# A hybrid decoder layer on one core: the last four gates as block pairs, and joined edits at the seams, in attention, at the feed-forward opening and at the last tokens

## The chip, the core and the metric

The kernel runs on one core of a Trainium2 chip. The metric is the device time of one execution in microseconds (us): the span from the first to the last instruction and the little that lies around it. The engines are named as the profile names them: PE is the matrix engine (TensorE) and PEld its weight loads, DVE the vector engine, ACT the scalar engine, POOL GpSimd, and SP the engine whose queue issues most DMA transfers; some are issued from ACT's queue.

## The reference, cut to what matters

The layer takes a prompt of 1024 tokens and eight single sample tokens; the kernel puts them side by side as 1032 columns (`TT`) of 1024 features. Everything is float32.

```python
def mixer_block(xn, mem_k, mem_v, ...):
    sc_b, sc_c, sc_x, z, xbc, dt_raw, q, gates = split(xn @ w_in)
    y_a = (sc_b * causal_conv(sc_c * sc_x)) @ w_sc_out                 # 1024 -> 1024
    xs, bm, cm = split(silu(causal_conv(xbc) + ssm_conv_b))            # 2048, 4x128, 4x128
    y_ssd, ssm_new = ssd_fn(xs, softplus(dt_raw + bias), a, bm, cm, s0)
    y_b = group_rmsnorm((y_ssd + ssm_d * xs) * silu(z)) @ w_ssm_out    # 2048 -> 1024
    y_c = softmax(q @ mem_k / 16) @ mem_v @ w_attn_o                   # 4 heads of 256, 256 memory tokens
    g_a, g_b, g_c = split(sigmoid(gates))                              # 3 x 1024
    return (g_a * y_a + g_b * y_b + g_c * y_c) @ w_merge_o, states

x = x + mixer_block(rmsnorm(x), ...)
x = x + (silu(h @ w_gate) * (h @ w_up)) @ w_down                       # h = rmsnorm(x), hidden size 2816
y = rmsnorm(x)
```

For the prompt `ssd_fn` is a scan over eight chunks of 128 tokens for each of four groups of eight heads; for each sample token it is one step of the recurrence from a given state, and its attention reads keys and values from a cache of its own. Outputs are `y`, the memory's keys and values, and the convolution and scan states.

## The kernel before, in words

**Layout and products.** Activations lie with 128 features on the partitions and the 1032 columns along the free dimension. A projection is computed in blocks of 128 output features. Each float32 operand is split into a rounded high part (an ACT copy) and a remainder (a DVE subtraction, `split_act` for activations, `weights` for weights), and each product of two operands is three products of TensorE: high by high, high by low, low by high.

**A plain block** (`gemm`, product at L195) covers the columns in three strips of 344. With 1024 input features (eight steps of `k`) that is 8 x 3 x 3 = 72 products. Between steps of `k` it calls `tick()`, which runs the next entry of the queue `pend`; `pace[0]` says how many entries a block takes. So other work (the scan, the attention) is emitted piece by piece between the products of plain blocks. `run_next` takes the next entry of its queues and, before it runs that one, issues the weight load of the one behind it if that is a `Step`.

**A pair of blocks** (`strassen`, products in `st_prod` at L240, two strips of 258 columns) computes two blocks of 128 features together with seven half-size products in place of eight: 168 products. Its inputs are sums and differences of quarter blocks of the activations (the forms B11, T1, nT2, B21, T3, B22, T4) and of the weights; the sums of the weights are made on DVE (`sa`, `sb`) and split (`st_split`) inside the pair. `st_early` computes the part with B11 and B21 of several blocks ahead of the other forms; their pairs then only need the rest.

**Stages in time.** The opening normalizes the input (to about 62 us). Three plain blocks follow (`xbc_tile(16)`, `xbc_tile(20)`, `z_step`), then the `z` pairs; beside these `pend` holds the memory's norm (`mem_rms`), its transposes (`mem_t`, half by half) and its keys and values (`kv_block`), 110 to 280 us. Until 971 us come the pairs of `xbc`, of the gates 0 to 19 (`gate_pair`) and of the short convolution, with steps of the sample recurrence beside them. `again` recomputes some activation forms from the stored input; the last pair, gates 18 and 19, has `plain` as its hook, which loads the first scan group and turns the forms back into plain activations.

Then the scan (971 to 1312 us). Its pieces fill `pend`, and the plain blocks that run beside it are twelve `fillers`, eight of `q` (`q_step`) and four of the gates 20 to 23 (`gate_step`, a plain block, a sigmoid on ACT, a store to `gt_d`), followed by the first eight output blocks (`outs`: `w_sc_out`, names `wo00` to `wo07`). `pace[0]` is the number of pieces divided by these twenty blocks; a chunk is `first` (transposes and masks), `second` (products `po`, L923, and `py`, L931, with the DVE steps at L927, L936 and L940) and `third` (state product `pss`, L949). After the last chunk of a group come its gating by `zs` (`z_pieces`, L1029), the sums for its norm (L1037) and the norm itself.

Beside attention (1370 to 1608 us) run the other sixteen output blocks: `wo10` to `wo17` and `wo20` to `wo27`, the two halves of `w_ssm_out`. Ahead of each run of eight, `out_in` loads the eight input blocks and splits them. An output block (`out_part`) loads its gate, multiplies the product by it (L1304), loads the sum so far (`mg_d`), adds and stores it. The attention's pieces, five for each block, are scores (`psa`, L1494) and softmax (L1415) for the prompt, probabilities transposed (`psp`, L1508), output (`a_out`), and the same for each sample (`s_query`, `s_keys`, `s_scores`: DVE products with sums, L1403, and so on). Then `w_attn_o` (`wo30` to `wo37`, to 1699 us) with the last gating and adding, `w_merge_o` (L1653, to 1795 us), the norm, five early blocks of the feed-forward part (`st_early`: gate 0, up 0, gate 2, up 2, gate 4; all but the first are stored in `e_d`), the pairs of its hidden features (to 2247 us), and the down projection. Its last part is done by columns: strips of 384, 384 and 264 columns (products at L1854 to L1856), each followed by `finish` for its three tiles of tokens: transposes (`psy`, L1830), squares on ACT, the scaling (L1839) and the store (L1840). The last tile holds the eight samples alone.

**What sets the order.** The text of the kernel is emitted once, and a list scheduler decides each engine's order from the dependences, under the marks that the text sets: `in_turn` keeps the load and split of weights in turn, and `tc.issue_after` puts an instruction behind a named one. Tiles come from pools with a fixed number of buffers, so a tile's load waits until an earlier holder is read. Loads by SP are issued in their order: a load that waits for its buffer holds those behind it.

## Time and profile before

| | us |
|---|---|
| runs of before | 2517.67, 2515.51, 2518.59 |
| their median | 2517.67 |
| the profiled execution, its own time | 2517.93 |
| its span, first to last instruction | 2516.0 |
| mean granted TensorE clock | 0.995 of full speed |

Busy time by stage of the profiled execution, for the stages that the prediction does not show:

| stretch, us | what | length | PE | DVE | ACT |
|---|---|---|---|---|---|
| 0 to 62 | opening | 62 | 44.81 | 37.90 | 40.01 |
| 280 to 971 | pairs ahead of the scan | 691 | 689.49 | 497.31 | 330.09 |
| 1608 to 1699 | `w_attn_o` | 91 | 90.48 | 44.96 | 22.06 |
| 1699 to 1795 | `w_merge_o` | 96 | 95.41 | 52.66 | 33.68 |
| 1842 to 2247 | hidden pairs | 405 | 404.28 | 217.74 | 138.59 |
| 2247 to 2463 | down projection | 216 | 215.84 | 70.25 | 36.55 |

How to read the rows: the lines of stretches in the prediction give start and end, length, then busy time and number of records for PE, PEld, DVE, ACT and POOL, the granted clock (1.00 is full speed), the busy share of the DMA engines and GB/s. A row of the chain of waits gives where a run of equal work starts, how long it holds the chain, its engine, and what it is. A wait row names who waits, for whom, then the time lost in us, how often, and the longest. A group's row gives line, engine, operation and tile, out<-in, then busy time and mean ns of one. A PE record is one pass of one product; a full float32 product leaves two records. "PE busy" is time in which a product is under way, and the waits of an engine that is not the bottleneck cost nothing.

### The profile page before, as it was taken

The numbers are of one execution on the slowest core, as the hardware profiler recorded it, in microseconds if no ns is written. First come the engines' busy times: TensorE is split into PE (matmuls) and PEld (weight loads), VectorE is DVE, ScalarE is ACT, GpSimd is POOL, SyncE is SP. The second block draws the span as 40 slices with busy tenths as digits, with TensorE's granted clock in tenths as the row PEclk, the third lists the DMA queues.
The fourth block names the chain that finished last, engine by engine and source line by source line (L and its number), as shares of the span: only waits on it lengthen the run. The fifth ranks groups of instructions, "written<-read, shape, count | busy, mean of one in ns | idle before, by whom it ended". The sixth has DMA issues, their size and how long they took to land.

```text
span 2516.0 us, 44833 instructions
## 1 busy us (share of the span) xinstructions
PE 2457.5 (98%) x18642; PEld 2391.0 (95%) x18642; DVE 1521.8 (60%) x2588; ACT 1040.5 (41%) x1679; POOL 139.1 (6%) x163
## 2 busy tenths in 40 slices
PE   7999999999999999999999999999999999999998
PEld 5999999999999998999989888999999999999998
DVE  6754586777677774776877762545775445463326
ACT  6553455353544535556544341213443333341102
POOL 0300000000000000321220000000000000000000
PEclk9999999999999999999999999999999999999999
DMA  6344434344344456666868987935442222273211
GB/s 201 101 147 156 126 102 152 110 128 125 110 135 135 127 157 195 193 209 226 299 214 281 319 262 231 316 120 160 139 143 85 85 69 93 71 248 128 76 34 68
DMA packets 348154, 394.71 MB, mean 157 GB/s; under 512 B 15414, under 2 KB 284838, under 8 KB 347943
## 3 DMA queue, kind: packets, MB, share of 16 engines
q1 hardware_dynamic: 328798, 338.90, 42.9%
q10 hardware_dynamic: 19153, 52.96, 5.6%
q8 instruction: 146, 2.39, 0.4%
q14 instruction: 57, 0.47, 0.1%
HBM read 283.57 MB, written 108.45 MB: 156 GB/s over the span
## 4 chain that ended last, share of the span: by engine, by line
PE 86%; DVE 6%; DMA 5%; ACT 2%; issue 1%; SPq 0%; DVEq 0%; ACTq 0%; POOL 0%
PE po L195 11%; PE pd L195 9%; PE ps_q L195 4%; PE pm L1653 4%; DMA kc<-in_cache_mem_k_dram 1%; PE py L931 1%; PE ps_g L195 1%; PE pss L949 1%; PE po L923 1%; PE ps_z L195 1%; PE X17m L240 1%; PE C3m L240 1%; PE G18m L240 1%; PE Z14m L240 1%; PE C6m L240 1%
## 5 line engine op out<-in xcount | busy, mean ns | idle before, releaser
L1795 DVE TENSOR_TENSOR x<-pd,x 128x1032 f32<-128x1032 f32 x24 | 29.6, 1232 | 130.7 <-PE pd L195 130.7
L878 ACT ACTIVATE r<-r,acum 128x128 f32<-128x128 f32 x256 | 78.8, 393 | 4.9 <-DMA r<-ac_d 4.5
L1304 DVE TENSOR_TENSOR gt<-po,gt 128x1032 f32<-128x1032 f32 x24 | 29.5, 1229 | 52.9 <-PE po L195 52.8
L910 POOL TENSOR_TENSOR xdd<-xdt,decst 128x512 f32<-128x512 f32 x32 | 44.7, 1397 | 295.1 <-DVE xdt L906 295.1
L649 DVE SCALAR_TENSOR_TENSOR ax<-u,prm,ax 128x1024 f32<-128x1024 f32 x44 | 56.3, 1280 | 0.1
L819 ACT ACTIVATE st<-st,es 128x128 f32<-128x128 f32 x128 | 41.7, 400 | 24.7 <-DMA st<-in_state_ssm_dram 19.9
L904 DVE TENSOR_TENSOR r<-r,cbm 128x1024 f32<-128x1024 f32 x32 | 39.0, 1218 | 8.8 <-ACT r L879 8.5
L821 DVE SCALAR_TENSOR_TENSOR st<-sr,dts,st 128x128 f32<-128x128 f32 x128 | 40.1, 345 | 0.4
L903 ACT COPY bT<-bp 128x128 f32<-128x128 f32 x32 | 8.5, 266 | 76.9 <-DVE cbm L901 76.9
L931 PE MATMUL py<-r,xdt 128*64 128x128 f32 x512 | 35.9, 283 | 4.2 <-issue 4.2
L927 DVE TENSOR_TENSOR yt<-po,ea 128x512 f32<-128x512 f32 x28 | 19.3, 691 | 34.0 <-PE po L923 34.0
L940 DVE SCALAR_TENSOR_TENSOR x<-x,dpar,yt 128x128 f32<-128x128 f32 x128 | 36.2, 345 | 0.2
L931 PEld LDWEIGHTS py<-r,xdt 128*64 128x64 f32 x512 | 28.0, 139 | 8.5 <-issue 5.1
L825 DVE SCALAR_TENSOR_TENSOR sr<-st,sr 128x128 f32<-128x128 f32 x128 | 35.3, 286 | 1.1
L879 ACT ACTIVATE r<-r 128x1024 f32<-128x1024 f32 x32 | 33.9, 1060 | 0.7
L949 PE MATMUL pss<-xdd,bT 128*128 128x512 f32 x64 | 33.7, 608 | 0.0
L1582 DVE TENSOR_TENSOR gt<-po,gt 128x1032 f32<-128x1032 f32 x8 | 9.9, 1233 | 38.4 <-PE po L195 38.4
L1660 DVE TENSOR_TENSOR x<-pm,xT 128x516 f32<-128x516 f32 x16 | 11.1, 695 | 35.8 <-PE pm L1653 35.8
L962 POOL TENSOR_TENSOR s<-s,cdec 128x512 f32<-128x512 f32 x28 | 32.2, 1149 | 0.5 <-DVE s L955 0.4
L1403 DVE SCALAR_TENSOR_TENSOR kc<-kc,qb 128x256 f32<-128x256 f32 x64 | 23.9, 419 | 13.7 <-DMA qb<-qs_d 7.9
L923 PE MATMUL po<-bc,s 128*128 128x128 f32 x224 | 29.5, 275 | 0.0
L923 PEld LDWEIGHTS po<-bc,s 128*128 128x128 f32 x224 | 28.4, 191 | 0.0
(9099 smaller groups left out, 8891.8 us busy)
## 6 DMA issues: line engine op xcount, KB each, us to landing
gt<-gt_d SPq DMA_DIRECT2D x32, 516.0 KB
r<-ac_d SPq DMA_DIRECT2D x32, 512.0 KB
mg_d<-gt SPq DMA_DIRECT2D x24, 516.0 KB
mg<-mg_d SPq DMA_DIRECT2D x24, 516.0 KB
xs_d<-ax ACTq DMA_DIRECT2D x22, 516.0 KB
hr<-h_d SPq DMA_DIRECT2D x22, 516.0 KB
gt_d<-G ACTq DMA_DIRECT2D x20, 516.0 KB
x<-xs_d SPq DMA_DIRECT2D x16, 516.0 KB
```

The lines of the kernel that those rows point to most:

```text
L195: PE.matmul(ps[:, n, :CW], wt[:, ks], x[:, n * CW : (n + 1) * CW], start=(k == 0 and i == 0), stop=(k == nk - 1 and i == 2),)
L240: PE.matmul(ps[:, n, :HC], wt[:, ks], x[:, n * HC : (n + 1) * HC], start=(start and kt == 0 and i == 0), stop=(kt == 3 and i == 2), skip_g ...
L649: V.scalar_tensor_tensor(acc[:, :T], u[:, j : j + T], w[j], acc[:, :T], op0=ALU.mult, op1=ALU.add)
L819: S.activation(st[:, i], st[:, i], AF.Copy, scale=es[:, g * 4 + i, b : b + 1])
L821: V.scalar_tensor_tensor(st[:, i], rb, dts[:, g * 4 + i, b : b + 1], st[:, i], op0=ALU.mult, op1=ALU.add)
L878: S.activation(r[:, j, :], r[:, j, :], AF.Relu, scale=-1.0, bias=acum[:, c, h : h + 1])
L904: V.tensor_tensor(r, r, bc(cbm.unsqueeze(1), [P, HPG, P]), op=ALU.mult)
L910: G.tensor_tensor(b3(xdd, HPG), b3(xdt, HPG), bc(decst[:, c, hs].unsqueeze(2), [P, HPG, 64]), op=ALU.mult)
L923: PE.matmul(po[:, t * P : (t + 1) * P], state["s"][:, t * P : (t + 1) * P], bcg[1][:, cs], start=True, stop=True,)
L931: PE.matmul(py[hp : hp + 64, (h // 2) * P : (h // 2 + 1) * P], xdt[:, h * 64 : (h + 1) * 64], r[:, (h % 2) * 4 + h // 2, :], start=True, s ...
L949: PE.matmul(pss, bT, xdd, start=True, stop=True)
L1653: PE.matmul(ps[:, n, :HC], wt[:, ks], x[:, half * HT + n * HC : half * HT + (n + 1) * HC], start=(k == 0 and i == 0), stop=(k == KD - 1 an ...
```

## The change

- **Gates 20 to 23** are no longer plain blocks beside the scan. `gate_pair(20)` and `gate_pair(22, plain)` follow `gate_pair(18)` ahead of the scan (18 and 20 now run before `again`); `gate_step` is gone. The scan has sixteen blocks beside it, so its pace is higher, and `marks` in `gemm` becomes a list, so that two pieces can fall on one step of `k`.
- **Seams between runs of blocks.** The inputs of the next run of output blocks are loaded and split inside the last block of the run before it (`out_ahead` puts a function into `seam`, which `gemm` calls at each `k`). Stores of an output block's result are put off to the second step of the next block (`owed`). The scan's pool moves to the right side of the memory.
- **Attention.** For the first half of `w_ssm_out` an output block now only copies the raw product (ACT) and stores it in `yr_d` from ACT's queue; for the second half it adds the raw product, multiplies the sum by the gate once and stores it in `yg_d`; it is added to the merged sum in the `w_attn_o` blocks. The sample's score steps (L1403) are ordered behind the scaled maximum of the softmax last emitted, and the sample's pieces start one place earlier, with an empty place in the middle. `q_rows` is called at once in place of through `pend`. The weights of `w_attn_o` are loaded one block ahead.
- **Seams in front.** In `strassen` the copy of the first quarter (`o11`) stands behind the split of the weights' sum; the memory's pieces get one more empty place behind `mem_rms`, and the two halves of `mem_t` become one piece; the weights of `xbc_tile(20)` are issued ahead of `xbc_tile(16)`.
- **Feed-forward opening.** A sixth early block, up 4, joins `st_early`.
- **Last tokens.** The strip of 264 columns becomes two: columns 896 to 1031 (token tile 7 and the samples), then columns 768 to 895 (tile 6), each followed by its own `finish`.

The diff, cut:

```diff
@@ -178,6 +178,9 @@
+    seam, owed = [], []
     def gemm(w, acts, name, width=P, off=0):
@@ -185,9 +188,14 @@
         pace[1] += pace[0] - n
-        marks = {nk * i // n for i in range(n)}
+        marks = [nk * i // n for i in range(n)]
+        between = seam.pop() if seam else None
         for k, (ah, al) in enumerate(acts):
-            if k in marks:
+            if between is not None:
+                between(k)
+            if k == 1 and owed:
+                owed.pop()()
+            for _ in range(marks.count(k)):
                 tick()
@@ -296,8 +304,7 @@
             prod(pa, wA, 0, "B11", True)
-            S.copy(h3(o11), hv(pa))
-        if early is not None:
+        else:
             tick()
@@ -308,6 +315,7 @@
             wS = st_split(sa, f"{nm}S")
+            S.copy(h3(o11), hv(pa))
         if ready is None:
@@ -353,12 +361,14 @@
     mg_d = dram("mg_d", [KD, P, TT])
+    yr_d = dram("yr_d", [KD, P, TT])
+    yg_d = dram("yg_d", [KD, P, TT])
     xs_d = dram("xs_d", [24, P, TT])
...
     h_d = dram("h_d", [NF, P, TT])
-    e_d = dram("e_d", [4, P, TT])
+    e_d = dram("e_d", [5, P, TT])
     q_d = dram("q_d", [8, P, TT])
@@ -701,15 +711,6 @@
-    def gate_step(i):
-        def s():
-            ps = proj(C_G + i * P, f"g{i}")
-            t = ev_tile(f"g{i}")
-            S.activation(t3(t), flat(ps), AF.Sigmoid)
-            S.dma_start(gt_d[i], t[:, :TT])
-        return [Step(wblock(w_in, C_G + i * P), f"wg{i}", s)]
     def xbc_conv(ct, u, name):
@@ -722,9 +723,9 @@
-    def xbc_tile(ct, name, ps=None):
+    def xbc_tile(ct, name, ps=None, w=None):
         if ps is None:
-            ps = proj(C_XBC + ct * P, name)
+            ps = gemm(w, xn, "ps_" + name)
         u = ev_tile("u" + name)
@@ -1138,9 +1139,10 @@
+    w_c0 = weights(wblock(w_in, C_XBC + 20 * P), "wC0")
     xbc_tile(16, "B0", ps_b0)
     make_forms(0)
-    xbc_tile(20, "C0")
+    xbc_tile(20, "C0", w=w_c0)
     make_forms(2)
@@ -1212,8 +1214,8 @@
     mem_load()
-    pend.extend([None, mem_rms])
-    pend.extend(lambda m=m, half=half: mem_t(m, half) for m in range(2) for half in range(2))
+    pend.extend([None, mem_rms, None])
+    pend.extend(lambda m=m: [mem_t(m, half) for half in range(2)] for m in range(2))
     pend.extend(lambda j=j, q=q: kv_block(j, q) for j in range(8) for q in range(2))
@@ -1245,6 +1247,8 @@
     assert not steps
+    gate_pair(18)
+    gate_pair(20)
     rb = ev_tile("rb")
@@ -1268,18 +1272,16 @@
-    gate_pair(18, plain)
+    gate_pair(22, plain)
     st_stack.close()
...
-    pool["ssd"] = ssd.enter_context(tc.tile_pool(name="ssd", bufs=2))
+    pool["ssd"] = ssd.enter_context(tc.tile_pool(name="ssd", bufs=2, side="right"))
     fillers = deque()
...
         fillers.extend(q_step(i))
-    for i in range(20, 24):
-        fillers.extend(gate_step(i))
@@ -1291,32 +1293,61 @@
     def out_in(src):
-        acts.clear()
-        for k in range(KD):
+        acts[:] = split
+        split.clear()
+        for k in range(len(acts), KD):
             if not ahead:
...
-    def out_part(w, m, gate, more, nm):
-        gt = ev_tile(f"gt{nm}")
-        SY.dma_start(gt[:, :TT], gt_d[gate])
+    def out_ahead(src):
+        for k in range(2):
+            out_load(src, k)
+        def between(k):
+            if k > 1:
+                split.append(split_act(ahead.popleft()[:, :TT], f"b0{k - 2}"))
+                out_load(src, k)
+        seam.append(between)
+    def out_part(i, m, w, src, nxt):
+        nm = f"{i}{m}"
+        if m == 0:
+            out_in(src)
+        if i != 1:
+            gt = ev_tile(f"gt{nm}")
+            SY.dma_start(gt[:, :TT], gt_d[(0, 8, 8)[i] + m])
+        if i == 2:
+            t = ev_tile(f"yr{nm}")
+            SY.dma_start(t[:, :TT], yr_d[m])
+        if m == KD - 1:
+            out_ahead(nxt)
         ps = gemm(weights(wblock(w, m * P), f"wo{nm}"), acts, f"po{nm}")
-        V.tensor_mul(t3(gt), flat(ps), t3(gt))
-        if more:
-            t = ev_tile(f"mg{nm}")
-            SY.dma_start(t[:, :TT], mg_d[m])
-            V.tensor_add(gt[:, :TT], gt[:, :TT], t[:, :TT])
-        SY.dma_start(mg_d[m], gt[:, :TT])
+        if i == 0:
+            V.tensor_mul(t3(gt), flat(ps), t3(gt))
+            owed.append(lambda: SY.dma_start(mg_d[m], gt[:, :TT]))
+        elif i == 1:
+            t = ev_tile(f"yr{nm}")
+            S.copy(t3(t), flat(ps))
+            S.dma_start(yr_d[m], t[:, :TT])
+        else:
+            V.tensor_tensor(t3(t), flat(ps), t3(t), op=ALU.add)
+            V.tensor_mul(t[:, :TT], t[:, :TT], gt[:, :TT])
+            owed.append(lambda: SY.dma_start(yg_d[m], t[:, :TT]))
+    split = []
     outs = deque()
-    for i, (src, w) in enumerate(
-        ((sc_d, a["w_sc_out"][0]), (yb_d, a["w_ssm_out"][0, 0:D]), (yb_d[8:16], a["w_ssm_out"][0, D : 2 * D]))
-    ):
-        outs.append(lambda src=src: out_in(src))
+    ins = ((sc_d, a["w_sc_out"][0]), (yb_d, a["w_ssm_out"][0, 0:D]), (yb_d[8:16], a["w_ssm_out"][0, D : 2 * D]), (at_d, None))
+    for i, (src, w) in enumerate(ins[:3]):
         outs.extend(
...
                 wblock(w, m * P), f"wo{i}{m}",
-                lambda w=w, m=m, i=i: out_part(w, m, (0, 8, 8)[i] + m, i > 0, f"{i}{m}"),
+                lambda i=i, m=m, w=w, src=src, nxt=ins[i + 1][0]: out_part(i, m, w, src, nxt),
             )
@@ -1331,15 +1362,13 @@
     while fillers or pend:
-        if len(fillers) == 2 and not ahead:
-            for k in range(2):
-                out_load(sc_d, k)
+        if len(fillers) == 1:
+            out_ahead(sc_d)
         run_next(fillers, outs)
     assert not fillers
-    pend.append(q_rows)
-    run_next(outs)
+    q_rows()
     flush()
@@ -1400,17 +1429,18 @@
                 c = slice(h * 256, (h + 1) * 256)
-                V.scalar_tensor_tensor(
-                    kc[:, c], kc[:, c], 1.0, qbs[b][:, c], op0=ALU.mult, op1=ALU.mult,
-                    accum_out=sc_s[:, m, b, h : h + 1],
-                )
+                with tc.issue_after(slot[0]):
+                    V.scalar_tensor_tensor(
+                        kc[:, c], kc[:, c], 1.0, qbs[b][:, c], op0=ALU.mult, op1=ALU.mult,
+                        accum_out=sc_s[:, m, b, h : h + 1],
+                    )
...
             V.tensor_reduce(mx[:npart, :n], sv, axis=AX.X, op=ALU.max)
-            V.tensor_scalar(mx[:npart, :n], mx[:npart, :n], -1.0 / 16.0, None, op0=ALU.mult)
+            ins = V.tensor_scalar(mx[:npart, :n], mx[:npart, :n], -1.0 / 16.0, None, op0=ALU.mult)
             for i in range(n):
@@ -1418,8 +1448,8 @@
             for i in range(n):
-                ins = V.tensor_scalar(pr[:, i, :], pr[:, i, :], sm[:npart, i : i + 1], None, op0=ALU.mult)
-            return ins
+                V.tensor_scalar(pr[:, i, :], pr[:, i, :], sm[:npart, i : i + 1], None, op0=ALU.mult)
+            return ins.ins
@@ -1496,7 +1527,7 @@
             heads[h][2][l2] = pr
-            return softmax(pr, ps, 2, P, nm)
+            slot[0] = softmax(pr, ps, 2, P, nm)
@@ -1539,9 +1570,9 @@
         for b in range(NS):
-            at_ = 4 + 5 * b
+            at_ = 3 + 5 * b
             for i, fs in enumerate(
-                ([(s_query, b), (s_keys, b, 0)], [(s_keys, b, 1)], [(s_scores, b, 0)], [(s_scores, b, 1)])
+                ([(s_query, b), (s_keys, b, 0)], [(s_keys, b, 1)], [], [(s_scores, b, 0)], [(s_scores, b, 1)])
             ):
@@ -1562,7 +1593,9 @@
         ph2 = ctx.enter_context(tc.tile_pool(name="ph2", bufs=1))
-        while outs:
+        assert not pend
+        outs.append(Step(wblock(a["w_attn_o"][0], 0), "wo30", None))
+        while len(outs) > 1:
             run_next(outs)
@@ -1574,11 +1607,17 @@
     for m in range(KD):
+        w = weights(wblock(a["w_attn_o"][0], m * P), f"wo3{m}")
+        if m + 1 < KD:
+            loaded[f"wo3{m + 1}"] = load_raw(wblock(a["w_attn_o"][0], (m + 1) * P), f"wo3{m + 1}")
         merged.append(big(f"mg{m}"))
         SY.dma_start(merged[m], mg_d[m])
+        yg = ev_tile(f"yg{m}")
+        SY.dma_start(yg[:, :TT], yg_d[m])
         gt = ev_tile(f"gt3{m}")
         SY.dma_start(gt[:, :TT], gt_d[16 + m])
-        ps = gemm(weights(wblock(a["w_attn_o"][0], m * P), f"wo3{m}"), acts, f"po3{m}")
+        ps = gemm(w, acts, f"po3{m}")
+        V.tensor_add(merged[m], merged[m], yg[:, :TT])
         V.tensor_mul(t3(gt), flat(ps), t3(gt))
@@ -1686,7 +1725,7 @@
     blocks = []
-    for i, (nm, j) in enumerate((("g", 0), ("u", 0), ("g", 2), ("u", 2), ("g", 4))):
+    for i, (nm, j) in enumerate((("g", 0), ("u", 0), ("g", 2), ("u", 2), ("g", 4), ("u", 4))):
@@ -1840,8 +1879,10 @@
     hl = [hs.pop(j) for j in js]
-    for n3 in range(3):
-        c0, c1 = 384 * n3, min(384 * n3 + 384, TT)
+    for n3, (c0, c1, tiles) in enumerate(
+        ((0, 384, (0, 1, 2)), (384, 768, (3, 4, 5)), (7 * P, TT, (7, 8)), (6 * P, 7 * P, (6,)))
+    ):
         w = c1 - c0
@@ -1856,7 +1897,7 @@
                 V.tensor_tensor(x2[m][:, c0:c1], ps[:, m - m0, :w], x2[m][:, c0:c1], op=ALU.add)
-        finish(range(3 * n3, 3 * n3 + 3))
+        finish(tiles)
```

1 line of the change is left out of this document (added).

## The prediction

> **What bounds the kernel now.** I read the page first: the busy shares, then the chain that ended last.
>
> ```profile
> span 2516.0 us, 44833 instructions
> PE 2457.5 (98%) x18642; PEld 2391.0 (95%) x18642; DVE 1521.8 (60%) x2588; ACT 1040.5 (41%) x1679; POOL 139.1 (6%) x163
> PE 86%; DVE 6%; DMA 5%; ACT 2%; issue 1%; SPq 0%; DVEq 0%; ACTq 0%; POOL 0%
> ```
>
> TensorE is busy 98% of the span and holds 86% of the chain. So time can leave only as products that are no longer computed or as one of the few holes between them. I therefore cut the span into stages (start and end, length, then busy time of PE, weight loads, DVE, ACT, POOL; clock; DMA).
>
> ```profile
> 110.00:280.00 170.00, 165.00 (x1375) 162.35 (x1374) 76.97 (x107) 77.61 (x126) 0.00 (x0) 1.00 0.46 144
> 971.00:1312.00 341.00, 334.42 (x2411) 306.46 (x2410) 233.13 (x392) 192.31 (x404) 80.77 (x66) 0.99 0.70 226
> 1312.00:1370.00 58.00, 54.11 (x348) 51.71 (x347) 41.50 (x50) 23.93 (x31) 2.05 (x2) 0.94 0.77 266
> 1370.00:1608.00 238.00, 229.27 (x1510) 211.33 (x1509) 128.99 (x307) 72.86 (x159) 0.00 (x0) 0.99 0.82 276
> 1795.00:1842.00 47.00, 43.87 (x359) 43.22 (x360) 42.57 (x70) 27.60 (x47) 0.00 (x0) 1.00 0.37 120
> 2490.60:2503.00 12.40, 12.22 (x99) 11.54 (x98) 10.63 (x35) 4.74 (x15) 0.00 (x0) 1.00 0.21 85
> 2503.00:2516.00 13.00, 3.78 (x25) 2.15 (x23) 8.71 (x29) 4.46 (x15) 0.00 (x0) 0.76 0.32 124
> ```
>
> In order: memory keys and values; the scan; its tail up to the first attention scores; attention and the output products beside it; the opening of the feed-forward part; the third column block of the last projection; what follows the last product. Holes of TensorE: 5.0, 6.6, 3.9, 8.7, 3.1, 0.2 and 9.2 us. The scan is the stage where DVE is nearest to TensorE (233 of 341 us).
>
> **The four gates.** The chain merges equal work; its rows give start, length, what and how many records.
>
> ```profile
> 890.49 20.23 PE B6m L240 x168
> 2247.16 215.50 PE pd L195 x1368
> 1271.44 2.21 PE po L195 x14
> 1273.65 0.89 PE po L923 x8
> 1274.54 1.02 PE py L931 x16
> 1277.11 0.93 PE pss L949 x2
> ```
>
> A pair by seven half products costs 20.23 us, so two pairs add 40.46 ahead of the scan. A plain block is 72 products of 344 columns at 215.50/1368 = 0.1575 us, 11.34 us; four of them leave the scan: -45.37. Net -4.9 us of products.
>
> But the four blocks were also cover. Six chunks of the scan's last group, 1271.44 to 1313.60, by DVE:
>
> ```profile
> 1271.44:1313.60 42.16, 42.16 (x326) 37.28 (x324) 34.30 (x65) 22.69 (x58) 12.28 (x12) 1.00 0.64 185
> DVE yt L927 <- PE po L923: 6.5, 6, 1.7
> DVE yt L936 <- PE py L931: 1.4, 4, 0.3
> 1320.32 4.66 DVE L1029 TENSOR_TENSOR x<-x,zs 128x1032 f32<-128x1032 f32 x4
> 1326.04 1.23 DVE L1037 TENSOR_TENSOR sqa<-sqa,zs 128x1032 f32<-128x1032 f32 x1
> PE po L195 <- DVE gt L1304: 3.9, 1, 3.9
> ```
>
> DVE is busy 34.30 and waits 7.9 for products of its own chunk: 42.2 of 42.16. A chunk thus takes 7.03 us by DVE's chain alone, whatever TensorE does beside it. TensorE's own part of a chunk is 0.89 + 1.02 + 0.93 = 2.84, about 3.6 with its transposes; the rest, some 20 block products, rides along. In the changed order three of the last group's chunks have no block product between them (those left wait for splits that stand behind the chunks on DVE). Each leaves 7.03 - 3.6 = 3.4 us open, some 2.5 of them fully: 8.5. Then DVE's gating of the last group (4.66, and two sums of 1.23 ahead of the next split halves: 7.1) has almost no products beside it. Against that, the 3.9 us wait at the old boundary goes, since the split is begun early. 8.5 + 7.1 - 3.9 is 11.7; I take +11. Bounds: +4 (only the chunks, half covered, less the 3.9) and +20 (three chunks, the gating, the norm behind it, nothing saved).
>
> **Attention.** The wait rows of 1370 to 1608:
>
> ```profile
> PE psp L1508 <- ACT pr L1415: 4.7, 3, 2.6
> PE psa L1494 <- ACT pr L1415: 3.3, 2, 1.8
> ```
>
> 8.0 of the 8.7 us stand behind the softmax. The score products of the sample now wait for the scaled maximum, so DVE serves the softmax first; eight gate products and eight additions (1.23 each, as L1037) leave DVE in this stage, and eight ACT copies with a store on ACT's own queue come in. I take -5, bounds 0 and -8.7. The store and later load of the raw half lie under products: DMA is at 0.82 here, and one transfer in ten goes away.
>
> **Seams in front.** Each pair beside a key/value block waits for its split sum (the first two rows, of 110 to 280, with the step that prepares keys and values in the third); the last two rows are those of the feed-forward opening, the same pattern.
>
> ```profile
> PE Z4m L240 <- DVE Z4Sl L228: 0.8, 1, 0.8
> PE Z6m L240 <- DVE Z6Sl L228: 0.6, 1, 0.6
> PE ps_mt L1179 <- DVE mem L1172: 1.0, 1, 1.0
> PE g0m L240 <- DVE g0e L327: 1.8, 1, 1.8
> PE g0e L240 <- ACT g2Eh L227: 0.9, 1, 0.9
> ```
>
> The eviction copy moves behind the cast of the sum, and the key/value step behind that: I take -4.5 of the 5.0, bounds 0 and -5. In the opening the sixth early block puts 48 products of 0.1204 (20.23/168), 5.8 us, where TensorE is open 3.1 us of 47 while DVE is busy 42.57. -2.5, bounds +1 (DVE also gets later sums) and -3.1.
>
> **The last tokens.** The third block of 264 columns becomes one of 136 and one of 128: 144 products where 72 were.
>
> ```profile
> 2502.06 0.29 PE L1856 MATMUL pl<-h20h,wl3l 128*128 128x264 f32 x1
> 2502.19 0.28 PE L1854 MATMUL pl<-h21h,wl3h 128*128 128x264 f32 x1
> 2502.31 0.29 PE L1855 MATMUL pl<-h21l,wl3h 128*128 128x264 f32 x1
> L1494 PE MATMUL psa<-kTh,q21h 128*128 128x256 f32 x8 | 2.5, 314 | 0.0
> 2502.92 1.36 PE L1830 MATMUL psy<-ident,x 128*128 128x128 f32 x8
> 2505.09 1.41 PE L1830 MATMUL psy<-ident,x 128*128 128x128 f32 x8 [0.81 <-DVE y L1834]
> 2508.50 0.75 DVE L1839 TENSOR_SCALAR y<-y,frs 128x1024 f32<-128x1024 f32 x1
> 2513.10 0.30 SPq L1840 DMA_DIRECT2D out_y_s_dram<-y  x1
> ```
>
> Starts 0.12 us apart: 72 x 0.121 = 8.7. What a product of split halves costs at 136 or 128 columns no row shows: none in the trace is narrower than the 256 of the scores. From below, by columns: 0.121 x 136/264 = 0.062 and 0.059, again 8.7 in all, +0. From above, the unsplit 128-column products of the scan: eight records, four products, in 0.89, that is 0.223 each; 0.237 at 136. 72 x (0.237 + 0.223) = 33.1, +24.4. One record of these, 0.112, lies between: 72 x 2 x 0.112 = 16.1, +7.4. The ends are far apart. The row nearest in width and in use of the array is the upper one, and every shape of split product in this kernel keeps to 256 columns or more, so no row speaks for the lower end. I take +24.4; nothing hides it, since TensorE is busy 12.22 of 12.40 there.
>
> The Trainium skill (TensorE: Matmul & The Clock Gate, "Back-to-back issue gap") gives about 81 ns for each weight-load-and-product at 128 columns in a steady stream and does not set these operands apart. By it the 144 products would take about 12 us, an estimate, +3, and the change would come out faster; no run here shows it yet, and it is the second case below.
>
> Behind the last product, two rounds of transposes, then the eight samples, end in the store at 2513.10. Now one tile alone is left, and its scaling (2508.50 even now, with the second tile's work between) is followed at once by its store: -4, bounds -3 and -6.
>
> **Sum.** -4.9 + 11 - 5 - 4.5 - 2.5 + 24.4 - 4 = +14.5. The profiled execution took 2517.93 (span 2516.0 and 1.93 around it), 0.26 over the median of 2517.67. 2517.67 + 14.5 = 2532.
>
> **The rivals.**
> *Narrow products stream by their columns.* Place: the last two column blocks. Price: 0.06 us, +0 in place of +24.4: 2532 - 24.4 = 2508, faster. It decides below the point where the sum is zero: (8.7 + 24.4 - 14.5)/144 = 0.129 us for one product. For it: 344, 264 and 258 columns cost 0.158, 0.121 and 0.120, little beside their columns. Against it: the 0.223 row, and that no such width occurs. If a product took one record of 0.112, the sum would be 14.5 - 24.4 + 7.4 = -2.5: 2515.
> *The scan becomes DVE's.* If the plain blocks now come too thin in earlier groups as well, every chunk drops behind DVE's 7.03 us: cover at +20 and attention at 0, since its loads and splits start late: 2532 + 9 + 5 = 2546. For it: DVE 233 of 341 us, of which 45 us go from TensorE and only 5 from DVE (four splits of 1.2). Against it: in the changed order all earlier chunks keep about 19 products each.
> *The seams do nothing.* If the holes in front are bound by the casts and not by order, 7 us stay: 2539. For it: DVE's 42.57 of 47; against: each wait names the split of the sum.
>
> **How the numbers follow.** Forecast 0.54, narrow by columns 0.21, one record of 0.112 each 0.07, DVE's scan 0.08, idle seams 0.10. The forecast's own range from its bounds is 2522 to 2543 (all ends together: 2519 to 2555). To leave out no more than 2 in 10 it must reach the faster case and a little past it, since that has bounds of its own: 2506 to 2546. A change of 0.2%, 5 us, is about what a measurement of this kernel tells from none. Faster: the second case (0.21), a part of the third (0.03) and a sliver of the first (0.02), 0.26. Within 0.2%: 0.08. Slower: 0.66.
>
> **What would show it.** The spacing of the 136- and 128-column products: 0.22 or 0.06 us, the two last blocks lasting some 37 or 13 us together with their transposes. The scan from its first transpose to the first scores: 399 us now, 354 were cover free, 365 forecast. TensorE waits in 1370 to 1608 behind the softmax under 4 us; in the pairs beside keys and values under 1; at the opening under 1. The last store about 9 us after the last product, 13 now to the end. The forecast is wrong if the narrow products cost under 0.13 us, or if the stretch up to the scores shrinks by less than 25 us.

## The result, and the profile after

The changed kernel took 2528.1 us (median of five runs, 2526.49 to 2529.95) against 2515.71 for the kernel before on the same chip: 12.4 us more, a ratio of 1.0046 with a 95% interval of 1.0032 to 1.0061. Slower, as forecast (2532 against 2517.67, +14.5). But the terms of the sum did not come out as priced; two of them missed by 14.5 and 12.9 us, in opposite directions.

The first lines of the changed kernel's page and its chain of waits:

```profile
span 2526.4 us, 45095 instructions
PE 2466.3 (98%) x18762; PEld 2400.2 (95%) x18762; DVE 1529.5 (61%) x2608; ACT 1047.9 (41%) x1694; POOL 126.9 (5%) x163
PE 90%; DVE 4%; DMA 3%; ACT 2%; issue 1%; SPq 0%; ACTq 0%; DVEq 0%; POOL 0%
```

TensorE is as busy as before and holds more of the chain, in a longer span. "Busy" hides what happened: a product at half the granted clock counts as busy too. The stages tell more. Each row below goes from the first product of one stage to the first of the next, read from the two timelines (us):

| stage | before | after | difference | forecast |
|---|---|---|---|---|
| start to the first `xbc` pair (memory's keys and values) | 280.3 | 276.2 | -4.1 | -4.5 |
| pairs ahead of the scan | 691.0 | 731.0 | +40.0 | +40.5 |
| scan to the first scores | 399.1 | 379.1 | -19.9 | -34.4 |
| first scores to `wo20` | 127.2 | 116.8 | -10.4 | -5 |
| `wo20` to `w_merge_o` | 201.9 | 201.4 | -0.5 | 0 |
| `w_merge_o` | 95.8 | 96.0 | +0.2 | 0 |
| opening and hidden pairs | 451.9 | 449.3 | -2.6 | -2.5 |
| down projection | 215.3 | 215.7 | +0.4 | 0 |
| last strips, first to last product | 40.3 | 51.8 | +11.5 | +24.4 |
| last product to the end | 13.2 | 9.1 | -4.1 | -4 |

They sum to +10.4, the difference of the two spans. Views of stretches of the changed kernel (columns as in the prediction): the scan with its tail; seven chunks of the second group; the change from the second group to the third; seven chunks of the last group; the tail; and two pieces at half the clock:

```profile
1007.17:1386.29 379.12, 355.34 (x2483) 321.38 (x2481) 269.81 (x438) 203.37 (x423) 70.71 (x68) 0.96 0.71 233
1112.90:1160.40 47.50, 47.50 (x366) 41.71 (x365) 38.94 (x72) 30.52 (x76) 18.33 (x17) 1.00 0.65 208
1160.40:1210.20 49.80, 45.98 (x274) 44.08 (x273) 32.66 (x42) 23.70 (x34) 1.44 (x3) 0.90 0.77 272
1294.70:1343.30 48.60, 42.75 (x324) 34.95 (x323) 39.45 (x73) 25.71 (x65) 15.90 (x15) 1.00 0.67 213
1343.30:1386.29 42.99, 32.86 (x195) 29.64 (x194) 32.12 (x38) 22.69 (x29) 0.40 (x1) 0.84 0.64 225
1174.00:1184.20 10.20, 10.20 (x42) 10.20 (x41) 5.28 (x10) 4.81 (x6) 0.19 (x1) 0.50 0.37 122
1348.10:1358.30 10.20, 5.86 (x20) 5.54 (x20) 10.20 (x9) 8.33 (x9) 0.00 (x0) 0.50 0.87 309
```

The same for the kernel before: the whole stretch, seven chunks of its second group, the change to the third, seven chunks of the last group, the tail:

```profile
971.27:1370.32 399.05, 388.58 (x2756) 357.99 (x2754) 274.80 (x442) 216.56 (x435) 82.82 (x68) 0.99 0.71 232
1084.00:1135.20 51.20, 51.17 (x389) 45.25 (x389) 36.72 (x70) 30.12 (x75) 18.13 (x17) 1.00 0.53 166
1135.20:1173.40 38.20, 37.77 (x257) 36.40 (x256) 22.51 (x33) 21.81 (x30) 0.12 (x1) 1.00 0.81 278
1268.00:1316.80 48.80, 48.80 (x376) 43.07 (x375) 37.80 (x72) 24.78 (x64) 15.30 (x15) 1.00 0.63 182
1316.80:1370.32 53.52, 49.63 (x319) 47.60 (x318) 38.40 (x44) 24.07 (x31) 0.00 (x0) 0.94 0.78 271
```

With 45 us of products fewer the chunks of the last group take 48.60 us in place of 48.80, and those of the second 47.50 in place of 51.20. In the second group TensorE is full both times; in the last it is now open 5.9 us. The change from the second group to the third has grown by 11.6. Behind one hole, and from within another, the clock stands at 0.50 for 10.2 us. Over the whole stretch it was 0.50 for 27.3 us, with TensorE busy in 23.0 of them; in the kernel before for 10.2 us, busy in 8.4. Half of that busy time is lost: 11.5 us in place of 4.2.

How the products lie shows best when one counts, on TensorE's timeline, the block products from the first `py` of a chunk to that of the next. The four groups have 28 such steps. In the changed kernel fifteen of them hold 19 block products and take 6.7 to 6.9 us, seven hold 22 to 26, three 17 or 18, and the last three hold 12, 0 and 0. In the kernel before thirteen hold 24 to 53 and take 7.6 to 12.5 us, and twelve hold 19. No step of either kernel is shorter than 6.4 us. A turn with no products at all is thus hardly shorter than one with 19, and with sixteen blocks the products run out before the last group ends. TensorE's waits in 1007 to 1386 of the changed kernel (who waits for whom, us in total, times, longest):

```profile
PE po L203 <- ACT b02h L162: 5.5, 2, 4.8
PE po L924 <- DVE s L956: 5.2, 3, 1.9
PE py L932 <- issue: 3.6, 1, 3.6
PE po L203 <- DVE b02l L163: 2.2, 1, 2.2
PE pskT L1412 <- DVE kTl L1415: 1.6, 1, 1.6
```

And a whole chunk of the last group on DVE's timeline (start, length, what; in brackets the idle time before and whom DVE waited for):

```profile
1328.38 0.68 DVE L956 TENSOR_TENSOR s<-pss,s 128x512 f32<-128x512 f32 x1
1330.32 0.69 DVE L928 TENSOR_TENSOR yt<-po,ea 128x512 f32<-128x512 f32 x1 [1.25 <-PE po L924]
1331.35 0.69 DVE L937 TENSOR_TENSOR yt<-py,yt 128x512 f32<-128x512 f32 x1 [0.34 <-PE py L932]
1331.96 0.28 DVE L902 TENSOR_TENSOR cbm<-bp,tri 128x128 f32<-128x128 f32 x1
1332.15 1.13 DVE L941 SCALAR_TENSOR_TENSOR x<-x,dpar,yt 128x128 f32<-128x128 f32 x4
1333.20 1.22 DVE L905 TENSOR_TENSOR r<-r,cbm 128x1024 f32<-128x1024 f32 x1
1334.34 0.68 DVE L907 TENSOR_TENSOR xdt<-xp,dtT 128x512 f32<-128x512 f32 x1
1334.94 0.68 DVE L956 TENSOR_TENSOR s<-pss,s 128x512 f32<-128x512 f32 x1
```

From one `s` to the next 6.56 us pass, and nothing but the chunk's own work is in them: `s`, then TensorE's `po` on it, then DVE through to the next `s`. It is a loop through both engines, and it lasts 6.56 us with no block product beside it at all. With seven chunks in 47.50 us, 6.8 each, the second group of the changed kernel runs at nearly that pitch too; TensorE is full there, so that row alone doesn't tell which engine sets it. The shorter chunk below does.

The other predicted signs: TensorE's waits at attention (1386 to 1613), ahead of the pairs beside keys and values, and at the opening, each the longest left:

```profile
PE psv L1557 <- ACT ot L1560: 2.2, 2, 1.3
...
PE ps_mt L1181 <- DVE mem L1174: 1.8, 1, 1.8
...
PE g0e L248 <- ACT g2Eh L235: 0.9, 1, 0.9
```

No wait behind the softmax (8.0 us before), none behind a split of a weights' sum, none of the opening's longer wait. And the last strips' products on TensorE's timeline:

```profile
2504.99 0.28 PE L1897 MATMUL pl<-h19h,wl3l 128*128 128x136 f32 x1
2505.10 0.28 PE L1895 MATMUL pl<-h19h,wl3h 128*128 128x136 f32 x1
2505.21 0.27 PE L1896 MATMUL pl<-h19l,wl3h 128*128 128x136 f32 x1
...
2517.10 0.27 PE L1895 MATMUL pl<-h21h,wl3h 128*128 128x128 f32 x1
2517.21 0.28 PE L1896 MATMUL pl<-h21l,wl3h 128*128 128x128 f32 x1
2517.32 0.28 PE L1897 MATMUL pl<-h21h,wl3l 128*128 128x128 f32 x1
...
2522.38 0.34 SPq L1879 DMA_DIRECT2D out_y_p_dram<-y  x1
```

They start 0.11 us apart at 136 and at 128 columns (median 0.112 over 65 and 69 such steps): one record each, neither 0.06 nor 0.22.

### The profile page after: what moved, and what is told of

Read it like the earlier page. It is cut to its first block, busy times and chain, and to the rows that moved or that the text cites. A ratio compares the mean times of both kernels' runs of the same rounds, so it can differ in the third digit from the quotient of the medians.

```text
span 2526.4 us, 45095 instructions
## 1 busy us (share of the span) xinstructions
PE 2466.3 (98%) x18762; PEld 2400.2 (95%) x18762; DVE 1529.5 (61%) x2608; ACT 1047.9 (41%) x1694; POOL 126.9 (5%) x163
## 4 chain that ended last, share of the span: by engine, by line
PE 90%; DVE 4%; DMA 3%; ACT 2%; issue 1%; SPq 0%; ACTq 0%; DVEq 0%; POOL 0%
PE po L203 12%; PE pd L203 9%; PE pm L1692 4%; PE ps_q L203 3%; PE py L932 1%; PE pss L950 1%; PE po L924 1%; PE ps_z L203 1%; PE B2m L248 1%; PE u20m L248 1%; PE g18m L248 1%; PE u14m L248 1%; PE g12m L248 1%; PE g8m L248 1%; PE g20m L248 1%
## 5 line engine op out<-in xcount | busy, mean ns | idle before, releaser
L820 ACT ACTIVATE st<-st,es 128x128 f32<-128x128 f32 x128 | 41.9, 394 | 21.9 <-DMA st<-in_state_ssm_dram 20.1
L911 POOL TENSOR_TENSOR xdd<-xdt,decst 128x512 f32<-128x512 f32 x32 | 33.4, 1044 | 329.0 <-DVE xdt L907 329.0
L1339 DVE TENSOR_TENSOR yr<-po,yr 128x1032 f32<-128x1032 f32 x8 | 9.9, 1232 | 54.0 <-PE po L203 54.0
L1621 DVE TENSOR_TENSOR gt<-po,gt 128x1032 f32<-128x1032 f32 x8 | 9.9, 1232 | 31.5 <-PE po L203 30.3
L662 DVE SCALAR_TENSOR_TENSOR ax<-u,prm,ax 128x1032 f32<-128x1032 f32 x22 | 28.3, 1286 | 0.0
```

The costliest lines, as they stand in the source:

```text
L820: S.activation(st[:, i], st[:, i], AF.Copy, scale=es[:, g * 4 + i, b : b + 1])
```

## The experiments

Ratios are against the kernel before, run beside it on the same chip, with the 95% interval.

**The four gates beside the scan again** (the changed kernel with `gate_step` back):

```diff
-    gate_pair(18)
-    gate_pair(20)
...
-    gate_pair(22, plain)
+    gate_pair(18, plain)
...
         fillers.extend(q_step(i))
+    for i in range(20, 24):
+        fillers.extend(gate_step(i))
```

> The changed kernel with the gates 20 to 23 as plain blocks beside the scan again (four fillers more, two pairs fewer), all else as changed. From the two profiles: the two pairs put 40.0 us ahead of the scan, the stretch from the scan's first transpose to the first scores became 19.9 us shorter, so the four gates cost 20.1. Theory (the scan lacks block products to cover its own chain): the time falls by about 20, to 2508. Rival (the longer stretch is the doing of the other edits there, the splits begun inside the last block and the changed pace, and not of the missing blocks): only the 45.4 us of plain products come back for the 40.0 of pairs, and the loss of 25 stays: about 2533.

2501.83 us against 2521.30, ratio 0.9916 (0.9902 to 0.9929): 19.5 us faster than the kernel before. The changed kernel had been 0.46% above it, so its four gates cost 1.3%, about 33 us by the ratios and 26.1 by the two profiles (2526.4 to 2500.3), not the 20.1 expected; the rival, 2533, is out. Beside the scan the profiles give 23.5 of it, and attention another 2.

**Both harmful parts undone** (the same, and the last strip whole):

```diff
-        ((0, 384, (0, 1, 2)), (384, 768, (3, 4, 5)), (7 * P, TT, (7, 8)), (6 * P, 7 * P, (6,)))
+        ((0, 384, (0, 1, 2)), (384, 768, (3, 4, 5)), (768, TT, (6, 7, 8)))
```

> The changed kernel with the gates 20 to 23 as plain blocks beside the scan and the last strip of 264 columns undivided. Theory: the two harmful parts, 20.1 and 7.4 by the profiles, leave, and what the seams in front (-4.1), attention (-10.5) and the opening (-2.6) bring remains: about 2500, 15 under the kernel before. Rival as in the run with the gates alone: 2526. If the gain at attention hangs on the shorter scan ahead of it, it is lost and the time is about 2511.

2496.09 us, ratio 0.9895 (0.9880 to 0.9910): 25.2 us faster than the kernel before, and the best version of this study. The gain at attention doesn't hang on the short scan. Its scan stretch, then attention up to `wo20`:

```profile
964.98:1359.83 394.85, 388.22 (x2771) 358.41 (x2770) 276.47 (x442) 217.46 (x437) 79.05 (x68) 1.00 0.72 236
1359.83:1474.51 114.68, 113.89 (x750) 108.59 (x748) 74.13 (x238) 57.69 (x132) 0.00 (x0) 1.00 0.70 235
```

**The gates alone, on the kernel before** (and the list of marks):

```diff
+    gate_pair(18)
+    gate_pair(20)
...
-    gate_pair(18, plain)
+    gate_pair(22, plain)
...
-    for i in range(20, 24):
-        fillers.extend(gate_step(i))
```

> The kernel before with the gates 20 to 23 as two pairs ahead of the scan, and the list of marks that the higher pace needs; nothing else. Theory (missing cover): slower by 20, about 2536. Rival (the loss comes from the seams' edits at the scan's end): the products saved remain, 4.9 less, about 2511.

2555.3 us, ratio 1.0133 (1.0114 to 1.0151): 34 us slower, more than the 20 expected. The loss does not come from the other edits at the scan; without them it is no smaller. Its stretch from the first transpose to the scores, shorter by 5.1 us only for 45 us of products fewer, at a clock of 0.94:

```profile
1010.83:1404.78 393.95, 357.35 (x2455) 321.84 (x2453) 268.81 (x438) 201.33 (x421) 70.35 (x68) 0.94 0.69 225
```

**The last strip alone, on the kernel before**:

```diff
-    for n3 in range(3):
-        c0, c1 = 384 * n3, min(384 * n3 + 384, TT)
+    for n3, (c0, c1, tiles) in enumerate(
+        ((0, 384, (0, 1, 2)), (384, 768, (3, 4, 5)), (7 * P, TT, (7, 8)), (6 * P, 7 * P, (6,)))
+    ):
```

> The kernel before with its last strip of 264 columns divided into 136 and 128; nothing else. By the changed kernel's profile a product of 136 or 128 columns takes 0.112 us, 144 of them 16.1 where 72 took 8.7, and the tail after the last product is 4.1 shorter; from the first product of this part to the end it was 7.4 longer: 2523. The prediction's own price (0.223 a product) would give 2536, streaming by columns 2512.

2528.3 us against 2521.3, ratio 1.0023 (1.0014 to 1.0032): 7.0 us slower, as the changed kernel's profile says, and neither +20 nor -4.

**Eighteen blocks** (the changed kernel, the last strip whole):

```diff
-    gate_pair(20)
...
-    gate_pair(22, plain)
+    gate_pair(20, plain)
...
+    for i in range(22, 24):
+        fillers.extend(gate_step(i))
```

> The changed kernel with the last strip undivided and the gates 22 and 23 as plain blocks: eighteen blocks beside the scan, 20 and 21 as a pair. With twenty blocks the same kernel was 25 us under the kernel before, with sixteen it would be about 5 above it less the strip's 7, so near +5. Theory (a chunk of the scan takes what its chain through DVE takes, so each block taken away comes back as a hole): half way, about 11 under before. Rival (a threshold: the first two blocks were not needed as cover): 20.0 us of pair for 22.7 of blocks, 28 under.

2500.53 us against 2522.77, ratio 0.9912 (0.9899 to 0.9926): 22.2 us faster, nearer to the rival. It isn't a matter of half and half. The stretch of this kernel:

```profile
986.37:1365.19 378.82, 367.89 (x2627) 336.87 (x2625) 272.12 (x440) 209.94 (x430) 75.79 (x68) 0.99 0.73 240
```

378.82 us with eighteen blocks, 379.12 with sixteen, 394.85 with twenty: taking two blocks (22.7 us) from twenty shortened the stretch by 16.0, taking the next two by nothing. There is a floor near 379 us. With eighteen blocks TensorE is open 10.9 us of the stretch and no chunk step holds fewer than 17 block products; with sixteen it is open 23.8, and the last steps run bare. The last pair then costs its full 20 us ahead of the scan.

**A shorter chunk** (the changed kernel, and a second one with twenty blocks; of the four steps that close a chunk on DVE three are left out, 0.85 us a chunk, so their `y` isn't the layer's and only the times are read):

```diff
-            for t in range(4):
+            for t in range(1):
                 V.scalar_tensor_tensor(
                     xg[t][:, cs], xg[t][:, cs], dpar[:, g * 4 + t : g * 4 + t + 1], yt[:, t, :],
```

> The changed kernel (sixteen blocks beside the scan), but of the four steps that close a chunk on DVE (L941, 1.13 us together) three are left out: 0.85 us less DVE in each of 32 chunks. Theory (the chunks follow DVE's chain): 28 intervals between chunks get 0.85 shorter, the scan 24 us, and the time is about 10 under before instead of 12 above. Rival (the loss is in the order of the block products, late splits and loads at the ends of groups): the chunks' own length doesn't decide, at most 5 are saved, about 8 above before.

2510.89 us against 2522.77, ratio 0.9962 (0.9950 to 0.9975): 11.9 under the kernel before where the changed kernel is 12 above it. The theory's 10 under holds, the rival's 8 above does not. The stretch and seven chunks of the second group:

```profile
1007.92:1370.11 362.19, 349.48 (x2483) 317.56 (x2482) 248.64 (x343) 204.40 (x424) 68.95 (x68) 0.98 0.75 242
1107.50:1150.30 42.80, 42.59 (x334) 36.51 (x333) 31.04 (x50) 28.10 (x74) 15.45 (x16) 1.00 0.58 175
```

A chunk fell from 6.8 to 6.1 us, the floor from 379 to 362. The commonest step, twelve of the 28, now holds 14 block products in place of 19 and takes 5.96 to 5.98 us, and none runs bare. So DVE's part of the loop decides how many products a turn takes in.

> The same three steps left out, with the gates 20 to 23 as plain blocks beside the scan (twenty blocks). There TensorE is busy 389 of 396 us in the stretch up to the scores. Theory: the products set the length there, and at most their 7 us of holes can go: 22 to 26 under before, where it was 20 under with the steps. Rival: if the chunks' chain alone sets the pace with twenty blocks as well, the scan shortens by 24 us here too: 43 under.

2506.84 us, ratio 0.9936 (0.9923 to 0.9948): 15.9 under, less than the 22 to 26 expected, and not faster than the same kernel with the steps (0.9916; the intervals overlap). Its seven chunks of the second group:

```profile
1079.80:1131.10 51.30, 51.13 (x388) 45.32 (x387) 34.33 (x51) 30.96 (x76) 17.32 (x17) 1.00 0.55 165
```

TensorE fills them (51.13 of 51.30), as in the kernel with the steps (51.2 us there). So with twenty blocks TensorE sets the length and three DVE steps less buy nothing; with sixteen they shorten the stretch by 17 us. Where this kernel came out above the one that does more work, part of it can be read: its stretch up to the scores is 398.4 us against 395.2, with a hole of 2.4 us that the load `x<-xs_d` ended and 3.4 us at a clock of 0.50 behind it. Why that load came late there stays open.

**The order in attention undone** (here and in the next three: twenty blocks, last strip whole):

```diff
-                with tc.issue_after(slot[0]):
...
-            at_ = 3 + 5 * b
+            at_ = 4 + 5 * b
...
-                ([(s_query, b), (s_keys, b, 0)], [(s_keys, b, 1)], [], [(s_scores, b, 0)], [(s_scores, b, 1)])
+                ([(s_query, b), (s_keys, b, 0)], [(s_keys, b, 1)], [(s_scores, b, 0)], [(s_scores, b, 1)])
```

> Twenty blocks beside the scan, last strip undivided, and in attention the sample's score steps no longer ordered behind the scaled maximum, its pieces at their old places. Theory of the prediction (what attention gains is the softmax served first): 7 of the 12.5 us that this stretch gained come back, 18 under before. Rival (the gain is DVE's relief by eight gate products and eight additions): it stays at 25 under.

2509.4 us, ratio 0.9941 (0.9929 to 0.9954): 13.4 under, 12 less than with the order. The stretch up to `wo20`, and its largest wait:

```profile
1363.68:1485.75 122.07, 114.44 (x749) 108.67 (x748) 78.66 (x257) 59.11 (x134) 0.00 (x0) 1.00 0.75 244
PE psa L1533 <- ACT pr L1453: 5.3, 3, 2.2
```

The stretch takes 7.4 us more than the 114.68 with the order, and 6.2 us of waits for the softmax came back (5.3, and 0.9 of `psp`). Of the rest of the two profiles' difference 3.5 us lie ahead of the scan, where the edit does nothing; the order is worth the 7.4, and that the whole 12 is its doing isn't shown.

**The gating and adding one by one** (no `yr_d` and no `yg_d`):

```diff
+        V.tensor_mul(t3(gt), flat(ps), t3(gt))
+        if i > 0:
+            t = ev_tile(f"mg{nm}")
+            SY.dma_start(t[:, :TT], mg_d[m])
+            V.tensor_add(gt[:, :TT], gt[:, :TT], t[:, :TT])
+        owed.append(lambda: SY.dma_start(mg_d[m], gt[:, :TT]))
```

> Twenty blocks beside the scan, last strip undivided, and the output blocks gated and added one by one into one sum as before (eight gate products, eight additions and their loads are back, the raw store is gone); seams and the order in attention as changed. Base: the same kernel with the raw store was 25 us under before. Theory (the order behind the scaled maximum is what serves the softmax; DVE's relief is worth little): 22 to 25 under. Rival (DVE's 20 us of work less make it): 12 to 18 under.

2513.32 us against 2520.32, ratio 0.9969 (0.9957 to 0.9980): 7.0 under, a loss of 18, more than even the rival gave. The stretch up to `wo20`, and the longest waits in it:

```profile
1365.89:1491.67 125.78, 116.27 (x735) 110.96 (x735) 88.13 (x252) 52.02 (x125) 0.00 (x0) 0.95 0.82 279
```

```profile
PE psa L1525 <- ACT pr L1445: 4.4, 1, 4.4
PE psp L1539 <- ACT pr L1445: 4.2, 1, 4.2
```

DVE is 14 us busier than with the raw store, the DMA share 0.82 instead of 0.70, and the waits for the softmax are back although the order stands. Which of the two, DVE's work or the transfers, brings them back isn't tested. Either edit alone leaves them; only together are they gone. Both runs are needed to see that.

**The splits at the start of a run**:

```diff
-        if m == KD - 1:
-            out_ahead(nxt)
...
-        if len(fillers) == 1:
-            out_ahead(sc_d)
+        if len(fillers) == 2 and not ahead:
+            for k in range(2):
+                out_load(sc_d, k)
```

> Twenty blocks beside the scan, last strip undivided, and the inputs of a run of output blocks split at the start of that run, with two loads ahead at the first run alone, as before. Base: 25 under before. Theory (the boundary's wait, 3.9 us in before, comes back at the second run, and less at the others): 19 to 21 under. Rival (the scan's own chain is late there, so the boundary is hidden or the early splits even delay the chunks): 25 under or more.

2520.62 us, ratio 0.9996 (0.9988 to 1.0005): the whole gain is lost, far beyond the theory's 4 to 6. The longest wait of 1320 to 1500:

```profile
PE po L203 <- ACT b00h L162: 11.1, 1, 11.1
```

The clock stood at 0.50 for 10.2 us, mostly within that wait:

```profile
1339.80:1350.00 10.20, 3.20 (x11) 3.01 (x12) 4.44 (x5) 3.67 (x4) 0.00 (x0) 0.50 0.85 284
```

The stretch up to the scores is 8.7 longer, attention up to `wo20` 15.9 (it holds 57 more product records, 9 us). It isn't the kernel before at this point, which waited 3.9 us. There three of the eight input loads were issued from 1328.85 us on, ahead of four stores of `yb_d`; here all eight stand behind such stores, from 1339.63 us on. So 25 us is what this arrangement loses without the early splits, not what they gain over the kernel before.

**The eviction copy back**:

```diff
             prod(pa, wA, 0, "B11", True)
+            S.copy(h3(o11), hv(pa))
...
             wS = st_split(sa, f"{nm}S")
-            S.copy(h3(o11), hv(pa))
```

> Twenty blocks beside the scan, last strip undivided, and in every pair the copy of the first quarter back at its old place, ahead of the split of the weights' sum. Base: 25 under before. Theory of the prediction (the waits of 0.5 to 0.8 us behind the sum's split, six of them beside keys and values, go by this copy): they come back, 20 to 22 under. Rival (the pieces of the memory, now one step later and joined, remove the waits): 24 to 25 under.

2500.97 us, ratio 0.9926 (0.9912 to 0.9940): 19.4 under, 6 us lost; 4.5 of them lie ahead of the first `xbc` pair (279.7 us against 275.1), and the waits are back, as the prediction had it:

```profile
PE Z4m L248 <- DVE Z4Sl L236: 0.8, 1, 0.8
PE Z2m L248 <- DVE Z2Sl L236: 0.6, 1, 0.6
```

**Half the weight columns** (each product of the two narrow strips as two of 64 weight columns, which changes the values of these strips; only the times are read):

```diff
+                    for half in range(1 if n3 < 2 else 2):
+                        n = P if n3 < 2 else 64
+                        kw = slice(ks.start + 64 * half, ks.start + 64 * half + n)
+                        pb = ps[:n, m - m0, 256 * half : 256 * half + w]
```

> The changed kernel, with each product of the strips of 136 and 128 columns cut into two of 64 weight columns (288 products in place of 144, and two DVE additions of 64 rows for each of 128). In the changed kernel a product of 136 columns and one of 128 both took 0.112 us. Theory (the floor is the load of 128 weight columns, as py's products with 64 columns at 0.064 each suggest): 0.056 to 0.064 each, 16 to 18 us in all, and the whole within 3 us of the changed kernel. Rival (a floor per product, whatever its weights): 0.112 each, 32 us in all, 16 us above the changed kernel.

2535.69 us (two runs), ratio 1.0061 (1.0043 to 1.0080), 4 us above the changed kernel's 1.0046 (the intervals overlap), and not 16. The products' timeline:

```profile
2526.56 0.23 PE L1899 MATMUL pl<-h21h,wl3h 128*64 128x128 f32 x1
2526.62 0.22 PE L1900 MATMUL pl<-h21l,wl3h 128*64 128x128 f32 x1
2526.68 0.22 PE L1901 MATMUL pl<-h21h,wl3l 128*64 128x128 f32 x1
```

0.060 us apart at 128 columns (median; 0.064 at 136), about half of 0.112. At these widths the price of a product goes with the number of its weight columns.

## Why the prediction was right, and where its steps failed

**The direction and the size** (2532 forecast, 2528.1 measured) came out of a sum in which two terms were wrong. By the prediction's own last line it failed on both counts: the narrow products cost 0.112 us, under 0.13, and the stretch up to the scores shrank by 19.9 us, under 25. That the total is near is luck.

**Cover, mis-sized: +11 forecast, +25.5 measured** (399.1 - 45.4 = 353.7 were cover free, 379.1 came). The holes themselves were nearly right in size and place. TensorE is open 23.8 us in place of 10.5, +13.3: the bare chunks at the end of the last group leave 7.3 (8.5 forecast), the tail behind them 8.6 (7.1), the old 3.9 is gone, and 3.8 between the second group and the third were not forecast (elsewhere it is some 2.5 less). The step that failed is that a hole was priced by its length alone. The clock fell behind and within the holes, which costs 7.3 us more than in the kernel before, and the forecast had no term for it. The other 4.9 us are products: 15 records more lie in the stretch than the four blocks would leave, 2.4 us at 0.158 (attention has 13 fewer); where the remaining 2.5 come from is open.

What makes the holes is the chunk's loop. It lasts 6.56 us where nothing else runs and 6.7 to 6.9 with 19 block products, so a chunk that gets fewer hardly ends earlier. Eighteen blocks still feed every turn; two fewer leave the last turns bare, and what they save comes back as holes and lost clock. The eighteen-block kernel (378.82) and the shorter chunk (362.19) show that floor and its cause. The rival in which the scan becomes DVE's priced the cover nearer (+20), but not by what came: it had every chunk drop behind DVE, and in the second group TensorE is busy 47.50 of 47.50 us. Its other half, attention at 0, was wrong.

The hole between the second group and the third comes from the first run of output blocks, which now starts there, as the trace reads: its splits on DVE and ACT stand between the group's gating and norm, and TensorE waits 2.8 us for `b02`. The change of groups takes 49.8 us instead of 38.2, with 17 records more in it and a dip of the clock. No run tests that by itself.

**Narrow products, mis-sized: +24.4 forecast, +11.5 measured.** The bound from the unsplit products (0.223, four products in eight records) was taken as the nearest row; the truth was its half, one record of 0.112. That price stood in the text as the value between, with a chance of 0.07. 144 of them are 16.1, +7.4 over the 8.7 of the whole strip. Of the other 4 us some 2.6 are the transposes of tile 7 and of the samples, which used to lie behind the last product and now lie ahead of it; transposes also wait 1.3 us more (1.5 in place of 0.2). So the tail's -4 was paid back here, and the run with the strip alone lost 7.0. The forecast's own rows held the answer: `py`, with 64 weight columns, takes 1.02/16 = 0.064 for a record, `po`, with 128, 0.89/8 = 0.111, both 128 columns wide. Another row of the kernel before says the same at a width of one column, with 128 weight columns:

```profile
L1050 PE MATMUL psny<-ones,sqa 128*128 128x1 f32 x72 | 8.3, 245 | 0.0
```

That is 8.3/72 = 0.115 for a record. From 1 to 136 columns the price goes with the weights, not with the width. The Trainium skill (TensorE: Matmul & The Clock Gate, "LDWEIGHTS (loading the stationary operand)") has the time of a weight load in ns as its columns over 1.2, by which 128 columns take an estimated 107 ns and 64 an estimated 53; the runs come near, with 0.112 and 0.060 us. The figure of the section that the prediction cited, 81 ns, does not hold for these operands.

**Attention, mis-sized: -5 forecast, -10.4 measured.** The mechanism was right (the softmax served first, no wait of TensorE left behind it). The bound of -8.7 took only the waits. From the first scores to `wo20` TensorE's open time fell from 8.7 to 2.4 us; 3.4 us at a clock of 0.50 are gone, worth 1.7, and 13 product records fewer, some 2 us, lie in the stretch. That the raw store was as necessary as the order was not seen.

**Right:** the pairs' own cost (+40.0 for +40.5), the seams in front (-4.1 for -4.5, and the copy's part shown by its own run), the opening (-2.6 for -2.5, no run of its own), the tail behind the last product (-4.1 for -4). Of the two that fell out, cover went 14.5 over and the narrow products 12.9 under: the total was right because they cancelled.

**The range** of 2506 to 2546 held the time. The forecast's own range, 2522 to 2543, did too, and the second case (narrow products cheap, 2508) would have been the wrong side: with the narrow price right and the cover as forecast the sum was -2.5.

## What to carry to other kernels

Before moving products out of a stage, find the loop that the rest of the stage runs in, through all its engines, and how long it lasts with nothing beside it; products may be taken away until the stage reaches that length, and no further. Count how many products a turn of the loop takes in (19 here): when the supply is short of that, the last turns run bare, and their holes can cost clock as well as length. A product with few columns costs what its weight columns do (0.112 us for 128 here), so cutting a strip pays only if the tail it shortens is worth more than a second set of loads. And two edits on one resource can each look worth the whole gain when taken away alone.

## What the runs showed of the hardware

A hole of TensorE can be paid twice. In the changed kernel the holes of 0.7 and 2.2 us around 1170 us were followed by 10.2 us at a granted clock of 0.50, and the one of 4.8 ahead of 1352 lay in another 10.2. TensorE was busy 10.20 and 5.86 us in them, so they cost 5.1 and 2.9. In the kernel with twenty blocks and the last strip whole, which has no hole above 1.1 us in this stretch but the 4.3 ahead of the first `py`, the clock was at 0.50 for 3.4 us in all. Not every hole brings a fall: with the order in attention undone, holes of 2.2 and 2.0 us passed, and the clock over that stretch is 1.00. The forecast had counted holes by their length alone.

The spacing of split products, in us: 0.120 at 258 columns, 0.112 at 136 and at 128, and 0.060 at 128 with half the weight columns.
